# Hybrid mixer trunk on one core: c spread in halves, four spare buffers in the early load ring, 8-step row blocks in the last output groups

## The chip, the cores and the metric

One core of a Trainium2 chip runs the whole program. The metric is device time in microseconds (us), median of several runs. Engines are named as the profile names them: PE (TensorE matmul), PEld (its weight loads), DVE (VectorE), ACT (ScalarE), POOL (GpSimd), SP (SyncE, which here issues the DMAs).

## What is computed

```python
c_act = silu(c)                                   # c: 1 x 2048
for l in range(2):
    mod = c_act @ w_ada[l] + b_ada[l]             # 2048 x 6144: shift, scale, gate
    h = rmsnorm(x, norm_g[l]) * (1 + scale) + shift          # x: 256 x 2048
    z = h @ w_in[l]                               # 2048 x 6656: thirteen pieces of 512
    o_fft = fourier_mix(f_x, w_fft[l]) * silu(f_g)
    o_na = neighbourhood_attention(...) * silu(na_g)
    o_ret = retention(...) * silu(r_g)            # both directions
    o_cv = conformer_conv(...) * silu(cv_g)
    y = concat(o_fft, o_na, o_ret, o_cv) @ w_out[l]          # 2048 x 2048
    x = x + gate * y
return rmsnorm(x, final_g)
```

Inputs and output are float32, and 256 MB of weights are read once.

## The kernel before

**Weights.** The program is a list of steps. A step loads one tile of 128x1024 floats (512 KB, `raw`) by SP. A *weight step* carries two blocks of 128 rows of `w_in` or `w_out`: ACT copies the tile to a rounded half `whi` (L321), DVE forms the remainder `wlo` (L322), and PE multiplies `hh*whi`, `hl*whi` and `hh*wlo`, where `hh` and `hl` are the two halves of the activations. In feature-major groups these are L338, L340, L341 (128x256 out), in row-major groups L367, L368, L369 (128x512 out, once for each half m of the 256 rows). An *ada step* multiplies a tile of `w_ada` (one output block of 128, one half of the 2048 inputs) by `cbc`, the spread silu(c), on DVE and sums it (L468).

**Rings.** `raw` has RAW = 8 buffers and `whi`/`wlo` WB = 4 pairs. Step n's turn issues the load of step n + 8, whose buffer is free when DVE has read it; weights are split up to four weight steps ahead. Each engine then works through its own list in order; a small number of instructions is put ahead by priority (AHEAD = 100), and `prep_x`, `prep_h`, `prep_rows` stand where steps call them.

**Start.** `warm` (L149) keeps PE busy with five matmuls of two passes each; four `cb` matmuls (L153), four tanh on ACT (L155) and four products on DVE (L156) make `cbc`; eight squares on ACT (L200) give the row sums, DVE and POOL make `rstd` (L205 to L207).

**Layer 0 in chunks.** The 16 blocks of 128 features of x are taken as chunks of 2, 3, 5 and 6 blocks (CH0), since a block of h needs its sums of `w_ada` first. While PE multiplies the weights of one chunk, DVE sums the ada tiles of the next. When the last of these is done, `mod_cols` (L1042 to L1044) makes the columns `mcol`, and `prep_h` makes `hh` (ACT, L271), a 32-bit `h` (ACT, L276) and `hl` (DVE, L284) out of the transposed rows `xt` (L231). Weights and ada steps are merged by a fixed rule, and the last few weight steps of a chunk (KEEP) come after all of them.

**Turnover.** `out_steps` makes four groups of 512 output columns. The last four weight steps of the last group form a unit *by rows* (`in_rows`): PE runs all of it for rows m = 0, then for m = 1, with weights kept in buffers of their own (ROW_TAGS). After m = 0, `half(0)` forms `yt` (L441), `xs` (L442) and its square, and then `turn_over(0)` runs: `rms`, and `prep_rows` for layer 1 (xn L243, transposes L245, `hh` L248, h L250 and L252, `hl` L254), while PE multiplies m = 1. The first four weight steps of layer 1 are a unit by rows as well. SPAN says between which weight steps of a stage the ada steps of a later one are placed: for the last out groups of layer 0 from step 1 to 7 before the end.

```python
while n_load < min(len(loads), n_run + RAW):
    loads[n_load].load()
if self is self.unit[-1]:
    g.half(0)
    for w in self.unit:
        w.rows(1)
```

Of the kernel before, what the change touches and what calls it, by code (L numbers as in the profile page):

```python
# [17 lines left out]
P = 128  # L18
# [73 lines left out]
def trunk(ctx, tc, x, c, cols, w_ada, w_in, w_fft, na_bias, consts, conv_w_pw, w_out, final_g, out):  # L92
# [42 lines left out]
    crow = sb.tile([P, DM], F32, tag="gate_bc", name="crow")  # L135
# [3 lines left out]
    nc.sync.dma_start(crow[0:1, :], c)  # L139
# [10 lines left out]
    for j in range(4):  # L150
        sl = slice(j * DG, (j + 1) * DG)
        b = bank("mx", "cb")
        T.matmul(b, one_row[0:1, :], crow[0:1, sl], start=True, stop=True)  # L153
        th = tb("cth")
        A.activation(th, b, AF.Tanh, scale=0.5)  # L155
        V.scalar_tensor_tensor(cbc[:, sl], th, 1.0, b, op0=ALU.add, op1=ALU.mult)  # L156
# [105 lines left out]
    def prep_h_(l, k0, n):  # L262
        for j0 in range(k0, k0 + n, 2):
# [9 lines left out]
            for k in range(w):  # L273
                kt = j0 + k
                if l == 0 or k < H32A:
# [15 lines left out]
    class Step:  # L291
        raw = None
# [3 lines left out]
        def load(self):  # L296
            self.raw = sb.tile([P, 2, DG], F32, tag="raw", name="raw", bufs=RAW)
            stream[0] = nc.sync.dma_start(self.src_view(), self.src)
# [4 lines left out]
    class Weights(Step):  # L303
# [10 lines left out]
        def split(self):  # L314
# [3 lines left out]
            else:  # L318
                self.hi = sb.tile([P, 2, DG], F32R, tag="whi", name="whi", bufs=WB)
                self.lo = sb.tile([P, 2, DG], F32R, tag="wlo", name="wlo", bufs=WB)  # L320
            A.activation(self.hi[:, :n], self.raw[:, :n], AF.Copy)  # L321
# [49 lines left out]
    def in_rows(steps, tags):  # L371

        for s, t in zip(steps, tags):
            s.unit, s.tags = steps, t

    class Group:
# [23 lines left out]
        def half(self, m):  # L400
            pass
# [26 lines left out]
    class OutGroup:  # L428
# [8 lines left out]
        def half(self, m):  # L437
            sl = slice(self.j * DG, (self.j + 1) * DG)
            with tc.high_priority(offset=AHEAD) if self.then else nullcontext():
                t = tb("yt")  # L440
                V.tensor_tensor(t, self.banks[m], GATE[self.l][:, sl], op=ALU.mult)  # L441
# [5 lines left out]
                if self.then:  # L447
                    self.then(m)

# [35 lines left out]
    def spread_gate(l, h):  # L485
# [6 lines left out]
        if h == 0:  # L492
            GATE[l] = sb.tile([P, DM], F32, tag="gate_bc", name="gate_bc")
        nc.gpsimd.dma_start(GATE[l][:, h * KH:(h + 1) * KH],
# [501 lines left out]
    def out_steps(l):  # L996
# [7 lines left out]
        in_rows(ws[-4:], ROW_TAGS[0])  # L1004
# [42 lines left out]
    def mod_chunk(l, k0, n):  # L1047
# [4 lines left out]
        both = mods(l, (0, 1), range(k0, k0 + n), done)  # L1052
# [21 lines left out]
    def turn_over(m):  # L1074
        rms(m)
        prep_rows(1, m, 0, 8)
# [34 lines left out]

    for m in range(2):
        for j in range(4):
            square_piece(m, j)
    rms(0, 1)

    loads = [s for s in steps if isinstance(s, Step)]
    weights = [s for s in steps if isinstance(s, Weights)]
    n_load = n_split = n_run = n_w = 0
    pos = {id(s): i for i, s in enumerate(loads)}  # L1120
    for s in steps:
        if isinstance(s, Step):
            while n_load < min(len(loads), n_run + RAW):
# [113 lines left out]
```

## Time and profile before

| | us |
|---|---|
| median of 3 runs | 974.92 (973.08 to 975.43) |
| the profiled execution | 971.75 |
| its span | 970.0 |
| PE busy | 908.0 |
| DVE busy | 781.3 |
| ACT busy | 591.9 |
| DMA read | 256.61 MB |

The span is what the profile's rows cover; the profiled execution's own time lies 1.75 us above it and 3.17 us under the median of the runs. PE is busy for 94% of the span, so what it loses is spread thin: the table of stretches shows, for each stage, how much of its length PE was not busy. A row of the timeline gives start, duration, engine, line and operation, and in brackets how long the engine had been idle before and what released it. A run of equal matmuls carries one row with its count.

### The profile page before, as it was taken

The page shows a single profiled execution, that of the slowest core. Times are in us where ns is not written, and L with a number is a line of the kernel's source. Part 1 is how long each engine was busy: PE and PEld are TensorE (multiplying, and loading weights), DVE is VectorE, ACT ScalarE, POOL GpSimd, SP SyncE. Part 2 cuts the span into 40 slices and gives each one's busy share as a digit, 9 for nine tenths or more (in the row PEclk, how much of TensorE's full clock was granted, in tenths as well). Part 3 has the DMA queues.
Part 4 walks back from the last instruction along what each step waited for, and adds up shares of the span by engine and source line. Part 5 has one row for each costly group of instructions (what it writes and reads, how often), then busy time and mean ns, then how long its engine had stood idle before and what let it go on. Part 6 is the DMA issues. An engine that isn't in the chain of part 4 may idle for free.

```text
span 970.0 us, 14749 instructions
## 1 busy us (share of the span) xinstructions
PE 908.0 (94%) x5298; PEld 771.2 (80%) x5298; DVE 781.3 (81%) x1269; ACT 591.9 (61%) x1027; POOL 19.6 (2%) x27
## 2 busy tenths in 40 slices
PE   4779799999998998999998999999999999999996
PEld 1668588889996777778886899999977889788784
DVE  5877698878999898987887689557987977578873
ACT  3477574579977766454463545668899844643451
POOL 1000000000000000010000000000000000010000
PEclk7889999999999999999999999999999999999998
DMA  9979899979788578888994799877665576379942
GB/s 348 349 267 335 296 333 354 345 270 347 235 305 292 179 245 291 258 295 314 335 334 146 250 357 396 278 243 233 219 214 178 156 245 229 110 233 320 327 161 87
DMA packets 109067, 259.69 MB, mean 268 GB/s; under 512 B 8385, under 2 KB 10561, under 8 KB 108737
## 3 DMA queue, kind: packets, MB, share of 16 engines
q1 hardware_dynamic: 108290, 256.64, 77.3%
q0 software_dynamic: 704, 2.11, 0.6%
q8 instruction: 41, 0.67, 0.3%
q14 instruction: 32, 0.26, 0.1%
HBM read 256.61 MB, written 2.11 MB: 267 GB/s over the span
## 4 chain that ended last, share of the span: by engine, by line
PE 65%; DVE 16%; DMA 9%; ACT 5%; issue 5%; POOL 1%; DVEq 0%; POOLq 0%; ACTq 0%
PE acc L368 11%; PE acc L367 10%; PE acc L369 10%; PE acc L341 9%; PE acc L338 8%; PE acc L340 8%; DVE wlo L322 6%; DMA raw<-in_w_ada_dram 5%; DVE raw L468 4%; DMA raw<-in_w_in_dram 3%; PE pwb L714 2%; ACT whi L321 1%; DVE cy L642 1%; DVE cy L626 1%; PE ff L810 1%
## 5 line engine op out<-in xcount | busy, mean ns | idle before, releaser
L321 ACT ACTIVATE whi<-raw 128x1024 fp32r<-128x1024 f32 (+1 forms) x272 | 277.1, 1028 | 174.2 <-PE acc L369 88.6
L322 DVE TENSOR_TENSOR wlo<-raw,whi 128x1024 fp32r<-128x1024 f32 (+1 forms) x272 | 319.4, 1181 | 62.1 <-ACT whi L321 60.3
L468 DVE CUSTOM_DVE_ANT_0 raw<-raw,cbc 128x1024 f32<-128x1024 f32 x192 | 232.5, 1219 | 45.5 <-DMA raw<-in_w_ada_dram 45.3
L338 PE MATMUL acc<-hh,whi 128*128 128x256 f32 x896 | 256.1, 287 | 13.4 <-ACT whi L321 6.4
L341 PE MATMUL acc<-hh,wlo 128*128 128x256 f32 x896 | 252.6, 285 | 4.6 <-DVE wlo L322 4.6
L340 PE MATMUL acc<-hl,whi 128*128 128x256 f32 x896 | 253.8, 284 | 1.4 <-DVE hl L284 1.4
L367 PE MATMUL acc<-whi,hh 128*128 128x512 f32 x600 | 241.7, 407 | 3.9 <-ACT whi L321 3.9
L368 PE MATMUL acc<-wlo,hh 128*128 128x512 f32 x600 | 240.2, 400 | 3.2 <-DVE wlo L322 3.1
L369 PE MATMUL acc<-whi,hl 128*128 128x512 f32 x600 | 238.5, 398 | 0.0
L338 PEld LDWEIGHTS acc<-hh,whi 128*128 128x128 f32 x896 | 171.5, 192 | 19.9 <-ACT whi L321 8.1
L341 PEld LDWEIGHTS acc<-hh,wlo 128*128 128x128 f32 x896 | 170.4, 192 | 6.9 <-DVE wlo L322 6.8
L340 PEld LDWEIGHTS acc<-hl,whi 128*128 128x128 f32 x896 | 171.6, 192 | 2.2 <-DVE hl L284 1.7
L367 PEld LDWEIGHTS acc<-whi,hh 128*128 128x128 f32 x600 | 113.6, 190 | 33.5 <-ACT whi L321 4.8
L368 PEld LDWEIGHTS acc<-wlo,hh 128*128 128x128 f32 x600 | 114.2, 190 | 32.7 <-DVE wlo L322 7.2
L369 PEld LDWEIGHTS acc<-whi,hl 128*128 128x128 f32 x600 | 114.0, 190 | 26.2
L417 ACT ACTIVATE z<-acc 128x512 f32<-128x512 f32 x99 | 57.4, 595 | 58.6 <-PE acc L341 31.8
L638 ACT ACTIVATE cvp<-uT,constants 128x256 f32<-128x256 f32 x160 | 70.4, 500 | 11.8 <-DVE cy L642 11.7
L642 DVE TENSOR_TENSOR cy<-cy,cvp 128x512 f32<-128x512 f32 x80 | 52.5, 684 | 1.6 <-ACT cvp L638 1.5
L200 ACT ACTIVATE junk<-xs 128x512 f32<-128x512 f32 x24 | 14.2, 592 | 40.1 <-DVE xs L442 40.1
L392 ACT ACTIVATE acc<-z 128x512 f32<-128x512 f32 x63 | 36.6, 598 | 0.3
L626 DVE SCALAR_TENSOR_TENSOR cy<-uT,constants,cy 128x256 f32<-128x256 f32 x80 | 34.6, 478 | 0.1
L231 PE MATMUL xt<-ident,xn 128*128 128x128 f32 x48 | 8.8, 315 | 11.7 <-DVE xn L226 11.7
(203 smaller groups left out, 703.5 us busy)
## 6 DMA issues: line engine op xcount, KB each, us to landing
raw<-in_w_in_dram SPq DMA_DIRECT2D x198, 512.0 KB, 5.1
raw<-in_w_ada_dram SPq DMA_DIRECT2D x192, 512.0 KB, 5.5
raw<-in_w_out_dram SPq DMA_DIRECT2D x64, 512.0 KB, 5.9
raw<-in_w_in_dram SPq DMA_DIRECT2D x20, 256.0 KB, 5.1
nab<-in_na_bias_dram SPq DMA_DIRECT2D x16, 192.0 KB, 3.6
xs<-in_x_dram SPq DMA_DIRECT2D x2, 1024.0 KB, 5.8
gate_bc<-gate_row POOLq DMA_DIRECT2D x4, 512.0 KB, 5.2
wsm<-in_w_fft_dram SPq DMA_DIRECT2D x4, 512.0 KB, 5.1
```

Of the source, the lines that this page charges most:

```text
L321: A.activation(self.hi[:, :n], self.raw[:, :n], AF.Copy)
L322: V.tensor_tensor(self.lo[:, :n], self.raw[:, :n], self.hi[:, :n].bitcast(F32), op=ALU.subtract)
L338: T.matmul(o, wh[:, sl], hh[:, k], start=fresh and blk % 2 == 0 and blk // 2 not in g.seeded, stop=False, skip_group_check=True)
L340: T.matmul(o, wh[:, sl], hl[:, k], start=False, stop=False, skip_group_check=True)
L341: T.matmul(o, wl[:, sl], hh[:, k], start=False, stop=en, skip_group_check=True)
L367: T.matmul(o, hh[:, k, sl], wh, start=st, stop=False, skip_group_check=m in g.seeded)
L368: T.matmul(o, hh[:, k, sl], wl, start=False, stop=False, skip_group_check=m in g.seeded)
L369: T.matmul(o, hl[:, k, sl], wh, start=False, stop=en, skip_group_check=m in g.seeded)
L417: A.activation(o, i, AF.Copy, scale=0.125 if last and self.piece == NAQ else 1.0)
L468: V.tensor_tensor_reduce(w, w, cbc[:, self.half * KH:(self.half + 1) * KH], 0.5, 0.0, ALU.mult, ALU.add, to)
L638: A.activation(d[:, i], uT[:, b + i, t:t + S], AF.Copy, scale=w[:, t, b + i:b + i + 1])
L642: V.tensor_tensor(y[:, b:b + 2], y[:, b:b + 2], d, op=ALU.add)
```

## The change

Five things:

1. `c` comes in two halves into two tiles of 128x1024, and is spread in two calls, `spread_c(0)` and `spread_c(1)`. The first chunk's ada steps are ordered by half, so that the first ones need only the first half of `cbc`. The warm matmuls go from 5 to 2; the row squares become four of 1024 elements in place of eight of 512, and `rms` is called among the ada steps.
2. `h` of the first chunk (k0 = 0) is made on DVE in place of ACT.
3. The load ring has four spare buffers (SPARE: two tiles of the gate, `yT`, `rk`, all unused so early) up to eight loads before the first step behind layer 0's third chunk (`n_early`). The tile `gate_bc` is split into two halves for it.
4. The last out group's eight weight steps are one unit by rows in place of the last four. The first four of them use the `whi`/`wlo` ring, so `held` puts off a split that would need a buffer of the unit before m = 1 has read it. The transposes for row half 0 of layer 1 are no longer called by `turn_over(0)` but by `between`, after four of the eight steps of m = 1.
5. SPAN of the last out groups goes from (1, 7) to (1, 9).

```diff
-    nc.sync.dma_start(crow[0:1, :], c)
+    for h in range(2):
+        nc.sync.dma_start(crow[h][0:1, :], c[:, h * KH:(h + 1) * KH])
...
+    spread_c(0)
...
-                if l == 0 or k < H32A:
+                if (l == 0 or k < H32A) and (l or k0):
...
+            if self.spare:
+                self.raw = sb.tile([P, 2, DG], F32, tag=self.spare, name="raw")
...
-                    for w in self.unit:
+                    for i, w in enumerate(self.unit):
+                        if i == 4:
+                            g.between()
                         w.rows(1)
+                    self.unit.clear()
...
+    def held(w):
+
+        return w.tags is None and len(ring) >= WB and any(ring[-WB] in u for u in holds)
...
+        def between(self):
+            if self.l < DEPTH - 1:
+                with tc.high_priority(offset=AHEAD):
+                    prep_rows(self.l + 1, 0, 0, 8)
...
-        in_rows(ws[-4:], ROW_TAGS[0])
+        in_rows(ws[-8:], (None,) * 4 + ROW_TAGS[0])
...
+        if k0 == 0:
+            both = [Ada(l, which, k, h) for h in range(2) for k in range(n) for which in range(2)]
+            both[-1].then = done
+            both.insert(2, Call(lambda: spread_c(1)))
+            both.insert(4, Call(lambda: rms(0, 1)))
...
         rms(m)
-        prep_rows(1, m, 0, 8)
+        if m:
+            prep_rows(1, m, 0, 8)
...
+    n_early = pos[id(tail[0])] - RAW
+    for i in range(n_early):
+        r = i % (RAW + len(SPARE))
+        if r >= RAW:
+            loads[i].spare = SPARE[r - RAW]
...
-            while n_load < min(len(loads), n_run + RAW):
+            while n_load < len(loads) and n_load < n_run + RAW + (len(SPARE) if n_load < n_early else 0):
...
-            while n_split < min(len(weights), n_w + WB) and pos[id(weights[n_split])] < n_load:
+            while (n_split < min(len(weights), n_w + WB) and pos[id(weights[n_split])] < n_load
+                   and not held(weights[n_split])):
...
+SPARE = ("gate0", "gate1", "yT", "rk")
...
-SPAN = ((2, 0), (1, 7), (8, 5), (3, 4), (1, 12))
+SPAN = ((2, 0), (1, 9), (8, 5), (3, 4), (1, 12))
-WARM = 5
+WARM = 2
```

How this moves instructions is read at three places. First, DVE at the start of the program, from `cbc` on. `ISA raw,msum<-raw,cbc` is an ada step, `ms` the row sum of `rms`, `xn` the normalized rows of the first chunk. Before:

```order
L156 SCALAR_TENSOR_TENSOR cbc<-cth,cb 128x512 x4
L468 ISA raw,msum<-raw,cbc 128x1024
L468 ISA msum 128x1
L205 TENSOR_REDUCE ms<-ssq 128x1
L206 TENSOR_SCALAR ms<-ms 128x1
L226 TENSOR_SCALAR xn<-xs,rstd 128x256
L468 ISA raw,msum<-raw,cbc 128x1024
```

And now:

```order
L159 SCALAR_TENSOR_TENSOR cbc<-cth,cb 128x512 x4
L210 TENSOR_REDUCE ms<-ssq 128x1
L211 TENSOR_SCALAR ms<-ms 128x1
L231 TENSOR_SCALAR xn<-xs,rstd 128x256
L496 ISA raw,msum<-raw,cbc 128x1024
L496 ISA msum 128x1
L210 TENSOR_REDUCE ms<-ssq 128x1
L211 TENSOR_SCALAR ms<-ms 128x1
L231 TENSOR_SCALAR xn<-xs,rstd 128x256
L496 ISA raw,msum<-raw,cbc 128x1024
```

The row sum and `xn` of the first row half have moved ahead of the first ada step, which still stands behind all four parts of `cbc`.

Second, ACT from the second weight step to the end of chunk 0's weights and on to chunk 1 (`z` and `uT` are evacuations of PE's sums). Before:

```order
L321 ACTIVATE whi<-raw 128x1024
L417 ACTIVATE z<-acc 128x512 x3
L321 ACTIVATE whi<-raw 128x1024
L417 ACTIVATE z<-acc 128x512
...
L417 ACTIVATE z<-acc 128x512 x3
L271 ACTIVATE hh<-xt,mcol 128x256 x2
L276 ACTIVATE h_469<-xt,mcol 128x256 x2
L271 ACTIVATE hh<-xt,mcol 128x256
L276 ACTIVATE h_475<-xt,mcol 128x256
L321 ACTIVATE whi<-raw 128x1024 x4
```

And now:

```order
L330 ACTIVATE whi<-raw 128x1024
L440 ACTIVATE z<-acc 128x512 x3
L330 ACTIVATE whi<-raw 128x1024
L440 ACTIVATE z<-acc 128x512
...
L440 ACTIVATE z<-acc 128x512 x3
L330 ACTIVATE whi<-raw 128x1024
L276 ACTIVATE hh<-xt,mcol 128x256 x2
L281 ACTIVATE h_466<-xt,mcol 128x256 x2
L276 ACTIVATE hh<-xt,mcol 128x256
L281 ACTIVATE h_472<-xt,mcol 128x256
L330 ACTIVATE whi<-raw 128x1024 x3
```

The copies to `whi` stand behind the same evacuations as before, except that the first one of chunk 1 has moved ahead of that chunk's `hh`.

Third, DVE at the turnover, from the split of layer 1's second weight step (`wyT`) to the first `xn` of layer 1. Before:

```order
L322 TENSOR_TENSOR wyT<-raw,wfx 128x1024
L322 TENSOR_TENSOR wlo<-raw,whi 128x1024 x3
L468 ISA raw,msum<-raw,cbc 128x1024
L468 ISA msum 128x1
L322 TENSOR_TENSOR wlo<-raw,whi 128x1024
L468 ISA raw,msum<-raw,cbc 128x1024
L468 ISA msum 128x1
L468 ISA raw,msum<-raw,cbc 128x1024
L468 ISA msum 128x1
L441 TENSOR_TENSOR yt<-acc,gate_bc 128x512
L442 TENSOR_TENSOR xs<-xs,yt 128x512
L468 ISA raw,msum<-raw,cbc 128x1024
```

And now:

```order
L331 TENSOR_TENSOR wyT<-raw,wfx 128x1024
L496 ISA raw,msum<-raw,cbc 128x1024
L496 ISA msum 128x1
L464 TENSOR_TENSOR yt<-acc,gate_bc 128x512
L465 TENSOR_TENSOR xs<-xs,yt 128x512
L331 TENSOR_TENSOR wlo<-raw,whi 128x1024
L210 TENSOR_REDUCE ms<-ssq 128x1
L211 TENSOR_SCALAR ms<-ms 128x1
L248 TENSOR_SCALAR xn<-xs,rstd 128x512
```

Of the three ada steps around `yt` of row half 0 one is left, ahead of it; one `wlo` now stands between `xs` and the row sum.

## Rows read from the trace of the kernel before

**Rows 1.** The page's first part: busy time of each engine, its share of the span, and its instructions.

```profile
PE 908.0 (94%) x5298; PEld 771.2 (80%) x5298; DVE 781.3 (81%) x1269; ACT 591.9 (61%) x1027; POOL 19.6 (2%) x27
```

**Rows 2.** The table of stretches, cut at the stages: chunk 0 (from 26.4), chunk 1, and the tail of layer 0 (262 to 420). Columns: stretch, its length, busy us and instructions of each engine, granted clock of PE as a share of full speed, DMA share, GB/s.

```profile
26.40:58.50 32.10, 22.86 (x144) 20.17 (x144) 24.14 (x45) 16.75 (x28) 0.00 (x0) 0.87 0.94 327
58.50:120.50 62.00, 54.43 (x313) 46.28 (x311) 46.30 (x72) 41.98 (x70) 0.00 (x0) 0.94 0.87 302
262.00:420.00 158.00, 150.41 (x872) 121.39 (x872) 144.95 (x273) 107.33 (x220) 4.08 (x6) 0.98 0.79 267
```

**Rows 3.** The same view for two stretches of 10 us in the early stages.

```profile
50.00:60.00 10.00, 5.85 (x23) 4.17 (x23) 7.57 (x16) 7.17 (x13) 0.00 (x0) 0.81 0.70 239
140.00:150.00 10.00, 10.00 (x86) 9.98 (x85) 8.52 (x14) 4.59 (x7) 0.00 (x0) 1.00 1.04 397
```

**Rows 4.** The view of waits: engine, line, what it waited for, us in total, times, longest. ACT, then PE, from 26.4 to 130; ACT from 130 to 199.1; SP's own queue from 0 to 260.

```profile
ACT z L417 <- PE acc L369: 15.5, 9, 5.1
ACT z L417 <- PE acc L341: 15.0, 9, 3.8
...
PE xt L231 <- DVE xn L226: 4.3, 2, 3.5
PE acc L338 <- ACT whi L321: 4.0, 3, 2.2
...
ACT whi L321 <- DMA raw<-in_w_in_dram: 7.3, 7, 1.9
...
SPq L298 <- DVE wlo L322: 109.6, 70, 5.6
```

**Rows 5.** The timeline at one weight step of chunk 0: start, us, engine, line, operation, and in brackets the idle time before it and its releaser.

```profile
35.98 0.60 ACT L417 ACTIVATE z<-acc 128x512 f32<-128x512 f32 x1 [2.22 <-PE acc L341]
...
36.48 1.05 ACT L321 ACTIVATE whi<-raw 128x1024 fp32r<-128x1024 f32 x1
...
37.58 0.39 PE L338 MATMUL acc<-hh,whi 128*128 128x256 f32 x1 [0.92 <-ACT whi L321]
```

**Rows 6.** The chain of waits, one piece in each line (start, us, what): the first piece after 26 us that is the transfer of a load.

```profile
281.73 5.71 DMA raw<-in_w_in_dram
```

**Rows 7.** The timeline of the start: the warm matmuls, those that spread c, the first ada step, the columns, and chunk 0's first matmuls.

```profile
1.61 6.26 PE L149 MATMUL warm<-warm 128*128 128x512 f32 x10 [1.61 <-DVE warm L146]
...
7.79 3.70 PE L153 MATMUL cb<-crow,one_row 1*128 1x512 f32 x8
...
12.76 1.22 DVE L468 CUSTOM_DVE_ANT_0 raw<-raw,cbc 128x1024 f32<-128x1024 f32 x1
...
25.09 0.16 DVE L1042 TENSOR_TENSOR mcol<-msum 128x4 f32<-128x4 f32 x1
...
26.36 0.80 PE L338 MATMUL acc<-hh,whi 128*128 128x256 f32 x2 [6.07 <-ACT hh L271]
...
28.59 0.58 PE L340 MATMUL acc<-hl,whi 128*128 128x256 f32 x1 [1.44 <-DVE hl L284]
```

**Rows 8.** The timeline at the start of chunk 1.

```profile
54.48 1.02 ACT L271 ACTIVATE hh<-xt,mcol 128x256 fp32r<-128x256 f32 x2
...
57.18 3.92 ACT L321 ACTIVATE whi<-raw 128x1024 fp32r<-128x1024 f32 x4
57.45 1.38 PE L231 MATMUL xt<-ident,xn 128*128 128x128 f32 x5 [3.50 <-DVE xn L226]
...
58.49 1.20 PE L367 MATMUL acc<-whi,hh 128*128 128x512 f32 x2
```

**Rows 9.** The timeline of the turnover: the split `wyT` and SP's two ada loads behind it; the first matmuls of m = 1; DVE's ada steps, `yt`, and `xn`; the transposes, and the matmul that waits for layer 1's first `hl`; the first feature-major matmul of layer 1.

```profile
499.23 1.22 DVE L322 TENSOR_TENSOR wyT<-raw,wfx 128x1024 fp32r<-128x1024 f32 x1
...
500.48 1.47 SPq L298 DMA_DIRECT2D raw<-in_w_ada_dram  x2
...
505.56 1.23 DVE L468 CUSTOM_DVE_ANT_0 raw<-raw,cbc 128x1024 f32<-128x1024 f32 x1 [1.66 <-DMA raw<-in_w_ada_dram]
...
509.68 0.39 PE L367 MATMUL acc<-wnav,hh 128*128 128x512 f32 x1
509.91 0.40 PE L368 MATMUL acc<-wona,hh 128*128 128x512 f32 x1
...
510.46 1.23 DVE L468 CUSTOM_DVE_ANT_0 raw<-raw,cbc 128x1024 f32<-128x1024 f32 x1 [1.39 <-DMA raw<-in_w_ada_dram]
...
511.61 0.69 DVE L441 TENSOR_TENSOR yt<-acc,gate_bc 128x512 f32<-128x512 f32 x1
...
515.78 0.88 DVE L243 TENSOR_SCALAR xn<-xs,rstd 128x512 f32<-128x512 f32 x2 [0.72 <-POOL rstd L207]
516.41 0.63 PE L245 MATMUL xt<-ident,xn 128*128 128x128 f32 x4 [1.96 <-DVE xn L243]
...
517.15 0.63 PE L367 MATMUL acc<-wcvA,hh 128*128 128x512 f32 x1
517.58 0.63 PE L368 MATMUL acc<-wcvU,hh 128*128 128x512 f32 x1
...
522.29 0.50 PE L369 MATMUL acc<-wnaq,hl 128*128 128x512 f32 x1 [1.95 <-DVE hl L254]
...
530.70 0.28 PE L338 MATMUL acc<-hh,whi 128*128 128x256 f32 x1
```

**Rows 10.** The timeline at the end: the last matmul.

```profile
960.22 0.39 PE L369 MATMUL acc<-wcvA,hl 128*128 128x512 f32 x1
```

More of the change, by code (lines that the diff above doesn't have):

```diff
@@ L134, in trunk @@
     xs = sb.tile([P, 2, DM], F32, name="xs")
-    crow = sb.tile([P, DM], F32, tag="gate_bc", name="crow")
+    crow = [wide(t, "crow") for t in ("gate0", "gate1")]
     cbc = sb.tile([P, DM], F32, name="cbc")
@@ L149, in trunk, with spread_c @@
         T.matmul(wb, warm[:, :P], warm, start=True, stop=True)
[L150 to L156, printed above, removed]
+    def spread_c(h):
+        for j in range(2):
+            sl = slice(h * KH + j * DG, h * KH + (j + 1) * DG)
+            b = bank("mx", "cb")
+            T.matmul(b, one_row[0:1, :], crow[h][0:1, j * DG:(j + 1) * DG], start=True, stop=True)
+            th = tb("cth")
+            A.activation(th, b, AF.Tanh, scale=0.5)
+            V.scalar_tensor_tensor(cbc[:, sl], th, 1.0, b, op0=ALU.add, op1=ALU.mult)
+    spread_c(0)
     mbias = pcol[:, 32:96].rearrange("p (l w k) -> p l w k", l=DEPTH, w=2)
@@ L291, in trunk @@
     class Step:
-        raw = None
+        raw = spare = None
         split = None
@@ L296, in load @@
         def load(self):
-            self.raw = sb.tile([P, 2, DG], F32, tag="raw", name="raw", bufs=RAW)
+            if self.spare:
+                self.raw = sb.tile([P, 2, DG], F32, tag=self.spare, name="raw")
+            else:
+                self.raw = sb.tile([P, 2, DG], F32, tag="raw", name="raw", bufs=RAW)
             stream[0] = nc.sync.dma_start(self.src_view(), self.src)
@@ L320, in split @@
                 self.lo = sb.tile([P, 2, DG], F32R, tag="wlo", name="wlo", bufs=WB)
+                ring.append(self)
             A.activation(self.hi[:, :n], self.raw[:, :n], AF.Copy)
@@ L374, in in_rows @@
             s.unit, s.tags = steps, t
+        holds.append(steps)
+    holds = []
+    ring = []
+    def held(w):
+        return w.tags is None and len(ring) >= WB and any(ring[-WB] in u for u in holds)
     class Group:
@@ L400, in half @@
         def half(self, m):
+            pass
+        def between(self):
             pass
@@ L440, in half @@
                 t = tb("yt")
-                V.tensor_tensor(t, self.banks[m], GATE[self.l][:, sl], op=ALU.mult)
+                V.tensor_tensor(t, self.banks[m], GATE[self.l, self.j // 2][:, (self.j % 2) * DG:(self.j % 2 + 1) * DG], op=ALU.mult)
                 V.tensor_tensor(xs[:, m, sl], xs[:, m, sl], t, op=ALU.add)
@@ L448, in half, with between @@
                     self.then(m)
+        def between(self):
+            if self.l < DEPTH - 1:
+                with tc.high_priority(offset=AHEAD):
+                    prep_rows(self.l + 1, 0, 0, 8)
         def done(self):
@@ L491, in spread_gate @@
         nc.gpsimd.dma_start(row, gcol[:, l, 8 * h:8 * h + 8])
-        if h == 0:
-            GATE[l] = sb.tile([P, DM], F32, tag="gate_bc", name="gate_bc")
-        nc.gpsimd.dma_start(GATE[l][:, h * KH:(h + 1) * KH],
+        GATE[l, h] = wide(f"gate{h}", "gate_bc")
+        nc.gpsimd.dma_start(GATE[l, h],
                             bass.AP(tensor=row.tensor, offset=row.offset, ap=[[0, P], [1, KH]]))
@@ L1050, in done @@
             prep_h(l, k0, n)
-        both = mods(l, (0, 1), range(k0, k0 + n), done)
+        if k0 == 0:
[3 more added lines that the diff above has]
+            both.insert(4, Call(lambda: rms(0, 1)))
+        else:
+            both = mods(l, (0, 1), range(k0, k0 + n), done)
         half = len(both) // 2
```

9 lines of the change are left out of this document (5 added, 4 removed).

## The prediction

> **What bounds the kernel now.** I read the engine shares first: PE is busy for 94% of the span [rows 1], so only what PE waits for, or runs at its lower clock, can be won. The table of stretches says where: chunk 0 has 9.2 us without PE (32.10 less 22.86), chunk 1 has 7.6 (62.00 less 54.43), the tail of layer 0 another 7.6, with DVE busy for 92% of it [rows 2]. Then the timeline of the turnover: from the first matmul of m = 1 at 509.68 to the first feature-major one at 530.70 pass 21.02 us, in which PE has 56 matmuls of 0.23 us (509.68 to 509.91) and 16 transposes of about 0.11, together 14.8. So 6.2 us are lost there [rows 9].
>
> The early losses decide what the spare buffers are worth, so I asked who comes last. Up to 130 us ACT waits for PE's sums (15.5 and 15.0 us) and never noticeably for a load; PE waits for ACT's `whi` [rows 4]. At one weight step it can be seen whole: ACT idles 2.22 us for a sum, evacuates it (35.98), and only then copies the next weight (36.48), which PE gets at 37.58 after idling 0.92 [rows 5]. The copy stands *behind the evacuation in ACT's list*. The chain of waits agrees: its first long piece after 26 us that is a load starts at 281.73 [rows 6]. Loads appear as ACT's last arriver only from 130 us on, 7.3 us in all [rows 4], where PE has whole stretches without a gap [rows 3].
>
> **The change part by part.** The sum is made against the profiled execution, 971.75 us, and then carried to the median, 3.17 above it.
>
> *Spread of c, squares, ada order.* Ten warm passes take 6.26 us [rows 7], 0.63 each; six fewer let the `cb` matmuls start up to 3.8 us earlier. Their eight passes take 3.70 at the rate of before; if PE then runs at half that rate, the fourth is done 3.7 later and nothing is won. I take 2, between them, since the warm row itself holds both rates. From that goes what the new order puts ahead of the first ada step: two sums, POOL's `rstd`, `xn`. The same sequence made DVE wait 0.72 for POOL at the turnover and its `xn` is 0.44 [rows 9], so with two short sums about 1.4, an estimate. But before, both such sequences stood among the eight ada steps: from 12.76 to 25.09 pass 12.33 us, and eight steps of the row's 1.22 at most need 9.8 [rows 7]. So 2.5 was spent there already, and now the same work is spent, only earlier. I take the columns 1.5 us earlier (bounds 3.8 and 0). What sets chunk 0 is not the first matmul (26.36) but the wait for `hl` at 28.59 [rows 7], and its `h` is now made on DVE, ahead of `hl`: two operations, each no longer than `xn`'s 0.44 for twice the width, 0.8 together. Term: -0.7, bounds -3 and +0.8. If it fails, the cover is ACT: it is idle there, and the copies wait for nothing else.
>
> *Chunk 1's first copy.* Before, PE idles 3.50 us for `xn`, does five transposes and starts at 58.49, one copy after 57.18, since ACT first did `hh` and `h` from 54.48 on [rows 8]. Now the first copy stands ahead of these and five transposes lie in PE's wait. The first matmul can start up to 2.4 us earlier; the other three copies end when they did, because ACT's work is the same, but the first step's 12 matmuls cover them. Eight transposes now lie behind these 12 matmuls, outside a wait: 0.9 at the price of above, up to 1.4 by the row's 1.38 for five [rows 8]. Term: -1.1, bounds -2.4 and +1.
>
> *Ring of 12.* A load issued earlier takes away a wait for a load. On the chain to 130 us there is none, and ACT's list keeps the copies where they were, behind the same evacuations. What SP waits for (109.6 us for DVE's reads [rows 4]) becomes less, and nobody waits for SP. Term: 0; the bound on the gain is the rival below. Bound on the other side: a spare tile must be free when the gate or the tail needs it; the last spare is used eight loads before that stage, so +0.5 at most.
>
> *Turnover.* m = 1 now has 48 matmuls, 11.2 us, in place of 24. The first transposes stand 21 matmuls (4.9 us) behind its start. DVE's chain to them is `yt` 0.69, `xs` about the same, one `wlo` (1.22, as `wyT`), two sums and the wait for POOL, `xn`: 4.1 us, with hand-offs up to 5.5. So of the 1.96 us of waiting about 0.5 stays: -1.5. The first use of layer 1's `hl` comes 29 matmuls and four transposes (some 7.2 us) behind the first transposes; before it came 5.9 behind and waited 1.95 [rows 9]: -1.7. At the lower clock a matmul takes 0.43 (517.15 to 517.58) in place of 0.23; that cost about 1.8 and goes if the waits get short: 0 to -1.8, I take -0.5. Against this, the same chain for row half 1, with three ada steps among it, now has 24 matmuls (5.6 us) before its transposes and needs 5.4 to 6.9: +1.5. Term: -2.2, bounds -4.5 and +1. What is late next is the ada step ahead of `yt`. Its load waits for the buffer that `wyT` frees: before, `wyT` ended at 500.45 and SP issued the two ada loads from 500.48 on, of which DVE had the first at 505.56 [rows 9], 5.1 us later. Now `wyT` should end about 5.5 us into the pass of m = 0 (four operations of `yt` and `xs` for the group before, 2.8, and two splits, 2.4). The load lands at 10.6, the step ends at 11.8, and `yt` can start at 11.6. It just fits.
>
> *Ends and the rest.* The last group of layer 1 ends with the same m = 1 matmul at 960.22 and the same row sums behind it [rows 10]: 0. Two halves of the gate, consts in one block, SPAN's two steps: off PE's chain, 0.
>
> Sum: -0.7 - 1.1 + 0 - 2.2 = **-4.0 us**: 967.75 for an execution like the profiled one, **971.0** as median (974.92 less 4.0, rounded up).
>
> **The rivals.**
>
> *The loads are the bound early, and the ring opens them.* SP waits most of the early time for a free buffer [rows 4], and the transfers move 327 and 302 GB/s in chunks 0 and 1 [rows 2] where 397 are possible, with 239 in one stretch [rows 3]. The 10.5 and 18.7 MB of these two stretches would pass at 397 in 73.6 us in place of 94.1. PE could give back at most what it idles there, 16.8 us. Then the time is 955 to 962. Against it: no last arriver of that chain is a load [rows 4 to 6]. [...]
>
> *The turnover only trades its waits.* The ada load takes 1 to 3 us more, `yt` and so the transposes come that much later, PE waits 2 to 3 us as before and falls to the lower clock: the turnover's term is 0, and -1.8 stays: 973.1. For it: the fit above has no slack, and the loads' medians differ by more than it. 27%.
>
> *The change doesn't do what it says.* `hl` of chunk 0 comes no earlier because `cb` runs at half rate and `h` loads DVE, the eight transposes cost what the moved copy wins, and the turnover trades waits: 974 to 975.5. 7%.
>
> *The pass of m = 0 drains the splits: slower.* By rows, a weight step lasts 6 x 0.233 = 1.40 us instead of 2.8, and DVE must deliver a remainder in each. If none were ready at the start, DVE would have eight of 1.22, `yt` and `xs` twice (2.8) and two splits of layer 1 (2.4) in 11.2 us: 15.0, so PE loses 3.8, the lower clock adds some 1.4, and in layer 1 the same pass loses 1.4. With the turnover's gain gone and the early -1.8 kept: +4.8, 979.7. It decides at about three remainders ready: then DVE's list fits. Against it: splits run four steps ahead, four of the eight have buffers of their own, and now no ada step lies among them. 9%.
>
> **How the numbers follow.** Forecast 50% (about 968 to 972.5), ring 7%, trade 27%, nothing 7%, slower 9%. I can tell the kernel from no change beyond about 0.3%, 2.9 us: under 972.0 is faster, over 977.8 slower. Faster: 0.46 of the forecast's 0.50, the ring's 0.07, 0.03 of the trade: 0.56. Slower: the drained pass's 0.09, and 0.01 of the rest: 0.10. Same: 0.34. The range leaves out the ring and most of the slow case: 966.0 to 976.0; its low end is the forecast with the turnover at -4.5 and the start at its better half, its high end the case of nothing with half a microsecond more.
>
> **What would show it.** Right: the wait for `hl` at chunk 0 under a microsecond earlier, chunk 1's first matmul 1 to 3 us earlier against the columns, ACT still without a noticeable wait for a load up to 130 us, DMA still near 300 GB/s in chunk 1; at the turnover less than a microsecond before the first transposes, and 56 + 24 matmuls' worth of work with some 4 us lost. Wrong: PE's gaps in chunks 0 and 1 shrink by many microseconds while GB/s rises; `yt` standing behind an ada step that waits for a load; PE waiting for `wlo` in the pass of m = 0.

## The result, and the profile after

969.26 us as median of 18 runs (964.74 to 973.68), against 975.37 for the kernel before (971.51 to 979.89, 18 runs): ratio 0.9935, 95% interval 0.9919 to 0.9951, so 6.1 us less by the medians (4.8 to 7.9 by the interval), where 4.0 were forecast. The profiled execution of after took 973.68 us, more than any other run of it, and that of before 971.75, less than all but one. The two traces are therefore compared stage by stage and not by their ends.

The page's first line of after is the same as that of before [rows 1] within 2 us:

```profile
PE 909.5 (94%) x5292; PEld 770.3 (79%) x5292; DVE 782.2 (80%) x1272; ACT 590.3 (61%) x1017; POOL 19.9 (2%) x27
```

The stretches of [rows 2], after:

```profile
26.40:58.50 32.10, 22.81 (x141) 19.78 (x142) 25.25 (x43) 15.34 (x24) 0.00 (x0) 0.99 1.03 395
58.50:120.50 62.00, 54.53 (x321) 46.13 (x320) 48.40 (x79) 44.39 (x75) 0.00 (x0) 0.95 0.88 310
262.00:420.00 158.00, 149.24 (x866) 119.96 (x866) 145.00 (x272) 107.28 (x220) 4.50 (x6) 0.99 0.80 267
```

In the first stretch the loads do run ahead, 395 GB/s in place of 327, and PE is busy for as long as before, 22.81 us and 22.86. Its clock, 0.99 in place of 0.87, is not to be compared; the last section says why.

The view of waits, ACT from 26.4 to 130, answers to [rows 4]: still the sums of PE, and 0.2 us for a load.

```profile
ACT z L440 <- PE acc L350: 16.6, 9, 5.3
ACT z L440 <- PE acc L381: 12.3, 8, 4.8
...
ACT whi L330 <- DMA raw<-in_w_in_dram: 0.2, 1, 0.2
```

The timeline of the start answers to [rows 7]. The eight `cb` passes last 7.19 us in place of 3.70, the first ada step starts 2.74 us later, the columns stand at 26.06, 0.97 later, and the wait for `hl` ends at 30.56, 1.97 later: PE idles 2.44 for it in place of 1.44, since DVE now makes `h` first. At the next weight step 0.55 comes back: five transposes now lie in PE's wait for `whi`, which is 0.37 in place of 0.92 [rows 5].

```profile
1.61 3.78 PE L150 MATMUL warm<-warm 128*128 128x512 f32 x4 [1.61 <-DVE ssq L1147]
5.32 7.19 PE L156 MATMUL cb<-crow,one_row 1*128 1x512 f32 x8
...
15.50 1.22 DVE L496 CUSTOM_DVE_ANT_0 raw<-raw,cbc 128x1024 f32<-128x1024 f32 x1
...
26.06 0.16 DVE L1069 TENSOR_TENSOR mcol<-msum 128x4 f32<-128x4 f32 x1
...
27.33 0.80 PE L347 MATMUL acc<-hh,whi 128*128 128x256 f32 x2 [8.36 <-ACT hh L276]
27.77 0.99 DVE L284 TENSOR_SCALAR h<-xt,mcol 128x256 f32<-128x256 f32 x2
...
30.56 0.58 PE L349 MATMUL acc<-hl,whi 128*128 128x256 f32 x1 [2.44 <-DVE hl L289]
...
37.81 0.71 PE L236 MATMUL xt<-ident,xn 128*128 128x128 f32 x5
38.88 0.39 PE L347 MATMUL acc<-hh,whi 128*128 128x256 f32 x1 [0.37 <-ACT whi L330]
```

Chunk 1 answers to [rows 8]. One copy now stands ahead of `hh`, and PE waits 1.63 for it, in place of 3.50 for `xn`; the eight transposes, five of which stood ahead of the first matmul, now come behind the first step's matmuls, from 62.02 on.

```profile
55.77 1.05 ACT L330 ACTIVATE whi<-raw 128x1024 fp32r<-128x1024 f32 x1
56.72 1.01 ACT L276 ACTIVATE hh<-xt,mcol 128x256 fp32r<-128x256 f32 x2
56.87 0.74 PE L379 MATMUL acc<-whi,hh 128*128 128x512 f32 x2 [1.63 <-ACT whi L330]
```

The turnover answers to [rows 9]. The one ada step ahead of `yt` is there at 504.58, after DVE idled 5.02 us for its load; `yt` follows at 505.73, 0.25 behind the end of PE's pass of m = 0. This is the order that the prediction gave as a sign of being wrong, but it cost PE little. The first transposes wait 0.51 in place of 1.96, and the first use of `hl`, at 518.53, waits no longer, where it waited 1.95. Two waits are new, both for row half 1 behind its transposes: 0.55 for `hh` and 0.20 for `hl`.

```profile
504.58 1.23 DVE L496 CUSTOM_DVE_ANT_0 raw<-raw,cbc 128x1024 f32<-128x1024 f32 x1 [5.02 <-DMA raw<-in_w_ada_dram]
505.73 0.69 DVE L464 TENSOR_TENSOR yt<-acc,gate_bc 128x512 f32<-128x512 f32 x1
...
510.89 0.63 PE L250 MATMUL xt<-ident,xn 128*128 128x128 f32 x4 [0.51 <-DVE xn L248]
...
518.53 0.39 PE L381 MATMUL acc<-wnaq,hl 128*128 128x512 f32 x1
...
524.97 0.50 PE L379 MATMUL acc<-wnaq,hh 128*128 128x512 f32 x1 [0.55 <-ACT hh L253]
...
526.58 0.50 PE L381 MATMUL acc<-wnaq,hl 128*128 128x512 f32 x1 [0.20 <-DVE hl L259]
```

The table of stretches, from the first matmul of m = 1 to the first feature-major one, in before and then in after: the granted clock was 0.92 and is 1.00, and the second stretch holds 18 more 128x512 matmuls.

```profile
509.68:530.70 21.02, 17.10 (x73) 12.75 (x72) 15.58 (x41) 9.14 (x24) 1.10 (x2) 0.92 0.49 160
```

```profile
505.32:525.54 20.22, 19.16 (x87) 14.87 (x86) 17.89 (x38) 10.96 (x22) 1.96 (x2) 1.00 0.66 203
```

### The profile page after: what moved, and what is told of

The parts are those of the page before. It is cut to its first block, busy times and chain, and to the rows that moved or that the text cites. A ratio compares the mean times of both kernels' runs of the same rounds, so it can differ in the third digit from the quotient of the medians.

```text
span 971.9 us, 14703 instructions
## 1 busy us (share of the span) xinstructions
PE 909.5 (94%) x5292; PEld 770.3 (79%) x5292; DVE 782.2 (80%) x1272; ACT 590.3 (61%) x1017; POOL 19.9 (2%) x27
## 4 chain that ended last, share of the span: by engine, by line
PE 63%; DVE 15%; DMA 10%; issue 6%; ACT 5%; POOL 0%; DVEq 0%; POOLq 0%; ACTq 0%
PE acc L380 10%; PE acc L381 10%; PE acc L379 10%; PE acc L350 9%; PE acc L347 9%; PE acc L349 9%; DVE wlo L331 6%; DMA raw<-in_w_in_dram 4%; DMA raw<-in_w_ada_dram 4%; DVE raw L496 3%; ACT whi L330 2%; PE pwb L741 1%; DMA raw<-in_w_out_dram 1%; PE cb L156 1%; PE ro L930 1%
## 5 line engine op out<-in xcount | busy, mean ns | idle before, releaser
L347 PEld LDWEIGHTS acc<-hh,whi 128*128 128x128 f32 x896 | 169.1, 189 | 21.3 <-ACT hh L276 8.8
L205 ACT ACTIVATE junk<-xs 128x512 f32<-128x512 f32 x16 | 9.5, 593 | 29.5 <-DVE xs L465 29.5
L464 DVE TENSOR_TENSOR yt<-acc,gate_bc 128x512 f32<-128x512 f32 x16 | 10.4, 684 | 12.5 <-PE acc L381 12.5
```

What stands on the lines that cost most here:

```text
L347: T.matmul(o, wh[:, sl], hh[:, k], start=fresh and blk % 2 == 0 and blk // 2 not in g.seeded, stop=False, skip_group_check=True)
```

## Experiments

Two marks from the timelines carry the comparison: **A**, the first matmul of layer 0's second feature-major run of 216 matmuls, 256.88 us in before and 255.98 in after; and **T**, the length from the first matmul of the row-major run that ends layer 0 (the out groups are most of it) to layer 1's first feature-major run of 192, 167.58 in before (389.31 to 556.89) and 166.22 in after. Up to A the two profiles of the changed kernel agree within 0.05 us at each stage's start. Behind it they part: the stage from 283 us on takes 65.08 us in one and 61.62 in the other. What lies there needs several profiles. A itself is not that firm between kernels: turn_ring and turn_ring_l0 run the same instructions up to it, and it stands at 255.74 and 258.29. So where it matters the stretch from chunk 0's first matmul to the second feature-major run of 72 is used as well, 57.10 and 56.98 in these two.

| kernel | median us | ratio to before | 95% interval | A | T |
|---|---|---|---|---|---|
| before | 975.37 | | | 256.88 | 167.58 |
| after | 969.26 | 0.9935 | 0.9919 to 0.9951 | 255.98 | 166.22 |
| after_again | 968.97 | 0.9953 | 0.9931 to 0.9976 | 256.00 | 166.93 |
| turn_alone | 970.14 | 0.996 | 0.9936 to 0.9983 | 256.81 | 166.91 |
| ring_alone | 972.5 | 0.9976 | 0.9953 to 0.9998 | 254.37 | 171.07 |
| start_alone | 975.4 | 1.0022 | 0.9997 to 1.0046 | 259.26 | 173.57 |
| turn_ring | 970.1 | 0.9928 | 0.9902 to 0.9954 | 255.74 | 169.02 |
| after_warm5 | 968.19 | 0.9919 | 0.9892 to 0.9946 | 255.71 | 167.18 |
| before_warm2 | 976.01 | 0.9988 | 0.9955 to 1.0022 | 253.94 | 175.03 |
| turn_ring_l0 | 965.25 | 0.989 | 0.9856 to 0.9924 | 258.29 | 164.65 |
| ring_old_order | 974.4 | 0.9976 | 0.9957 to 0.9994 | 258.03 | 173.22 |
| after_ms_first | 966.66 | 0.9898 | 0.9874 to 0.9923 | 254.58 | 165.57 |
| best_new_start | 967.99 | 0.993 | 0.9899 to 0.9961 | 254.66 | 168.63 |
| best_old_start | 966.93 | 0.9924 | 0.9898 to 0.995 | 258.61 | 167.68 |

Each ratio is against runs of the kernel before on the same chip (medians 973.76 to 976.10).

**The three parts alone.** All three are the changed kernel with the other parts put back; c stays in two transfers. Their ratios multiply to 0.9958, 4.1 us less.

turn_alone:

```diff
     spread_c(0)
+    spread_c(1)
...
-                if (l == 0 or k < H32A) and (l or k0):
+                if l == 0 or k < H32A:
...
+        both = mods(l, (0, 1), range(k0, k0 + n), done)
...
+            square_piece(m, j)
+    rms(0, 1)
...
-SPARE = ("gate0", "gate1", "yT", "rk")
+SPARE = ()
...
-WARM = 2
+WARM = 5
```

> The turnover alone: the last output groups in 8-step row blocks, the transposes called between them, and SPAN (1, 9); the ring stays at 8 and the start is as before (c comes in two transfers, both halves spread at once). My theory: 2.2 us faster than the kernel before (bounds 4.5 faster to 1 slower), and between yt of row half 0 and the first feature-major matmul of layer 1 the loss of 6.2 us falls to about 4. The rival in which the whole gain is the turnover: about 6 us faster. The rival in which the turnover only trades its waits: 0.

Measured 3.9 us less (interval 1.7 to 6.2, which holds the theory's 2.2 and the first rival's 6, and not 0), A unchanged, T shorter. With the block of four steps T is 167.58, 171.07, 173.57, 175.03 and 173.22 us, mean 172.1; with eight in layer 0, nine profiles between 164.65 and 169.02, mean 167.0. The profile that the forecast was made from was the shortest of five and lies among the nine. What splits cleanly is the part of T that the turnover holds, from the last out group's first matmul on: 63.81 (before) to 67.78 with four steps, mean 66.47; 60.84 (after) to 63.33 with eight, mean 61.72. The first transposes wait 1.96 (before) to 4.27 us in the five, 0.51 to 0.63 in the nine.

How the wait grows with four steps is visible in the timeline of before_warm2, whose turnover is that of before. Three ada steps stand around `yt`, and they wait for loads whose buffers come free behind `wyT`. That split ended 9.4 us ahead of the end of PE's pass of m = 0 in before and 7.3 ahead here; the ada step ahead of `yt` waits 1.64 for its load where it waited 1.39, `yt` starts 4.27 us behind the pass in place of 1.77, and the transposes wait 4.27, where [rows 9] had 1.96.

```profile
512.54 1.23 DVE L497 CUSTOM_DVE_ANT_0 raw<-raw,cbc 128x1024 f32<-128x1024 f32 x1 [1.64 <-DMA raw<-in_w_ada_dram]
...
513.69 0.69 DVE L465 TENSOR_TENSOR yt<-acc,gate_bc 128x512 f32<-128x512 f32 x1
...
518.31 1.09 PE L251 MATMUL xt<-ident,xn 128*128 128x128 f32 x4 [4.27 <-DVE xn L249]
```

With eight steps one ada step is left there. DVE idles 4.8 to 6.1 us for its load in the nine profiles, and `yt` starts 0.04 to 1.29 us behind the pass; the wait is 0.63 in turn_alone, with the latest `yt`, and 0.56 in after_ms_first. It did not follow the load.

ring_alone has the start as above, SPARE as changed, and the turnover of before:

```diff
-        in_rows(ws[-8:], (None,) * 4 + ROW_TAGS[0])
+        in_rows(ws[-4:], ROW_TAGS[0])
...
-        if m:
-            prep_rows(1, m, 0, 8)
+        prep_rows(1, m, 0, 8)
...
-SPAN = ((2, 0), (1, 9), (8, 5), (3, 4), (1, 12))
+SPAN = ((2, 0), (1, 7), (8, 5), (3, 4), (1, 12))
```

> The four spare buffers alone, with the start and the turnover as before. My theory: 0 (within 1 us), since ACT's copies stand behind the same evacuations and none of them waits for a load up to 130 us. The rival in which loads bound the early stages: 4 us faster or more, with the gaps of PE in chunks 0 and 1 shorter and more GB/s in chunk 1 than 302.

Neither. By the ratio 2.3 us are won (0.2 to 4.6), and A is 2.5 us earlier (254.37), more than the theory and less than the rival had. Nor does the rival's way of winning show: chunk 0's stretch has 388 GB/s and the same three waits of PE for `whi`, 0.92 each, and chunk 1's has 310. What differs is the list: ACT's first copy of chunk 1 is ahead of `hh` here too.

```profile
55.21 1.05 ACT L331 ACTIVATE whi<-raw 128x1024 fp32r<-128x1024 f32 x1
56.16 1.01 ACT L277 ACTIVATE hh<-xt,mcol 128x256 fp32r<-128x256 f32 x2
56.31 0.73 PE L380 MATMUL acc<-whi,hh 128*128 128x512 f32 x2 [1.63 <-ACT whi L331]
```

A split is issued only for a weight whose load has been issued (`pos < n_load`); a longer ring lets it be issued earlier, and so puts it earlier in ACT's list.

start_alone keeps the new start, with that turnover and SPARE empty:

> The start alone: c spread in halves, the order of the first ada steps, two warm matmuls, the squares of 1024 elements, h of chunk 0 on DVE, and the copy ahead of chunk 1's hh if it comes with them; ring of 8, turnover as before. My theory: 1.8 us faster (bounds 4 faster to 1 slower), the columns of chunk 0 1.5 us earlier. The rival in which the start is worth nothing, because PE runs at its lower clock through the spread of c and DVE has h to make: 0, with the columns no earlier than before.

The rival has it: the `cb` passes ran at their low rate (7.19 us), the columns are 0.97 later, and the ratio, 1.0022, doesn't exclude zero. A is 2.4 us *later*: 0.97 at the columns, 1.0 at the first `hl`, less the 0.55 of the next weight step, and 0.8 in four feature-major runs behind 85 us, whose equal matmuls are slower (see Addresses).

after_again (no edit):

> The changed kernel once more, for a second profile, since the first one on record is 4 us above its median. If the theories of the three parts are right and add up, it is as fast as the sum of the three parts alone, about 6 us under the kernel before. A place where the first profile was late and this one is not is chance; a place where both are late is the program.

Its ratio's interval, 2.3 to 6.7 us less, holds both 4.0 and 6.1, and the 4.1 of the three parts. At A the two profiles agree within 0.02 us; the first one's late places, from 283 us on, are chance by the rule of the expectation.

**Loads or list.** ring_old_order has the ring of 12, but splits are issued as with 8:

```diff
-            while (n_split < min(len(weights), n_w + WB) and pos[id(weights[n_split])] < n_load
+            while (n_split < min(len(weights), n_w + WB) and pos[id(weights[n_split])] < min(n_load, n_run + RAW)
```

> The ring of 12 alone as in the run with the ring alone, but a weight may be split only when a ring of 8 would have let it: the loads run ahead with 12 buffers, while ACT's and PE's lists up to 130 us are again those of the kernel before. Theory A (the ring's gain of 2.5 us up to 256 us is the place of chunk 1's first copy in ACT's list, not the loads): PE's first matmul of the second feature-major run of 72 stands at about 85.5, half a microsecond behind the kernel before (85.01) as its start does, and by 256 us nothing is won. Rival B (earlier loads are what helps): 83.5 there and 254.4 at the run of 216, as with the ring alone.

85.55 and 258.03: theory A. The lists of PE and ACT are those of before up to 150 us. From chunk 0's first matmul to that run pass 58.86 us, 58.66 in before and 56.61 in ring_alone; over all profiles 58.1 to 59.3 in the five with the copy behind `hh`, 56.4 to 57.5 in the nine with it ahead. With 385 GB/s in chunk 0, PE waits for `xn` at chunk 1 as in [rows 8], and ACT's copies are again behind `hh`:

```profile
54.94 1.02 ACT L277 ACTIVATE hh<-xt,mcol 128x256 fp32r<-128x256 f32 x2
...
57.63 3.93 ACT L331 ACTIVATE whi<-raw 128x1024 fp32r<-128x1024 f32 x4
57.91 1.38 PE L237 MATMUL xt<-ident,xn 128*128 128x128 f32 x5 [3.50 <-DVE xn L232]
```

Its ratio is nevertheless as low as ring_alone's, 0.9976, with an interval (0.9957 to 0.9994) that leaves out 1. So beyond A something of the longer ring may help (the tail of layer 0 starts with more loads issued); the spread of single profiles there hides it, and it stays open.

**The start.** turn_ring puts the whole start back, as in the first edit above, and keeps ring and turnover:

> The changed kernel with the start put back as it was: c spread at once, five warm matmuls, eight squares, h of chunk 0 on ACT, ada steps in their old order; ring of 12 and turnover as changed. Theory A (the start costs some 2 us, the ring's gain is chunk 1's copy that moves ahead of hh, the turnover gives 2 to 4): faster than the changed kernel by 1 to 3 us, 6 to 9 under the kernel before; the ring's 2.5 us at 256 us into the span stand in the trace in full, not the 0.9 of the changed kernel. Rival B (the start is worth nothing either way, its late columns are made up for by the ring): as fast as the changed kernel, within 1 us.

0.9928: it can't be told from the changed kernel, so theory A's 1 to 3 us are not shown and rival B is not excluded. A is 255.74, not 254.4: here the passes of the five warm matmuls were slow for longer (7.50 us in all) and the columns stood at 26.33, 0.74 later than in ring_alone, which is about half of the difference. after_warm5 and before_warm2 change one number:

```diff
-WARM = 2
+WARM = 5
```

> The changed kernel with five warm matmuls in place of two, nothing else. Theory A (the two warm matmuls end before PE's passes get short, so the eight cb passes take 0.86 us each and push the first ada step behind): the cb passes take 0.43 each again, the columns of chunk 0 come 0.5 to 1.5 us earlier than 26.06. A second point: in the profiles of kernels with the new start, long stretches of equal matmuls later on (614 to 694 us) take 81.45 us in place of 80.54. If that comes from the number of PE's instructions ahead, it goes here; if it comes from another part of the start, it stays at 81.45.

The columns come at 25.36, 0.70 earlier, and the `cb` passes take 0.43 each. The stretch of 672 stays at 81.45.

> The kernel before (with c in two transfers) with two warm matmuls in place of five. Theory A: cb passes at 0.86 us each, chunk 0's columns 1 to 2 us later than 25.09, and the time 1 to 2 us longer. Rival B (the warm matmuls can go, the spread of c has slack behind the squares): columns at 25.1, same time. The second point as in the run with five: 81.45 or 80.54 us from the first of the 672 equal matmuls to the next row-major group.

A miss: here two warm matmuls were *better* in the profile, and the time, 0.9988, is the same. The `cb` passes started at 5.32 as in after and took 3.82 us in all, and the columns stood at 24.12. (The edit is one number, but DVE's list moved with it: the row sum and `xn` now stand ahead of the first ada step here too.) So two warm matmuls are a matter of chance. PE's passes begin at 0.85 us and become 0.43 at a moment that differs from profile to profile; where it came before the end of `cb`, it came between 5.0 and 7.6 us, and the two warm matmuls end at 5.3. Of seven profiles with two, `cb` ran at 0.43 in two (before_warm2, after_ms_first) and at 0.85 in five (after twice, start_alone, best_new_start, best_old_start); with five warm matmuls it ran at 0.43 in all seven. In the five slow ones PE was busy from 1.61 to 12.51 us without the change; why is open. The timeline's row of `cb`, in best_new_start and then in after_ms_first:

```profile
5.32 7.19 PE L156 MATMUL cb<-crow,one_row 1*128 1x512 f32 x8
```

```profile
5.32 3.86 PE L156 MATMUL cb<-crow,one_row 1*128 1x512 f32 x8
```

**Addresses.** In the four profiles with the new start as changed (after twice, start_alone, after_warm5), equal matmuls were slower later on: from the first of the 672 to the next row-major group 81.45 us, against 80.54 in the others. after_ms_first moves addresses alone:

```diff
+    small("ms", 1)
     junk = wide("nak", "junk")
```

> The changed kernel with the four small tiles ms given their place in memory ahead of the tile for the squares, as they had before. No instruction changes and none moves; only the addresses of raw, whi and wlo move by 128 bytes, so that they stand to hh and hl as in the kernel before (modulo 4096). Theory A (the 1% by which equal matmuls are slower in the four profiles with the new start comes from the addresses): 80.54 us from the first of the 672 equal matmuls to the next row-major group, 57.31 for the stretch before, and 2 to 3 us less in all. Rival B (it comes from something else in the new start): 81.45 and 57.66 to 57.76, same time as the changed kernel.

80.54 and 57.31, as theory A had it, and 0.9898: no instruction differs. (The time is not the addresses' alone to show: best_new_start below, with the same addresses, is at 0.993.) The timelines of after, then of after_ms_first, at both ends of the stretch:

```profile
612.00 0.28 PE L347 MATMUL acc<-hh,whi 128*128 128x256 f32 x1
...
693.45 0.40 PE L379 MATMUL acc<-whi,hh 128*128 128x512 f32 x1
```

```profile
607.48 0.28 PE L347 MATMUL acc<-hh,whi 128*128 128x256 f32 x1
...
688.02 0.39 PE L379 MATMUL acc<-whi,hh 128*128 128x512 f32 x1
```

**Versions.** turn_ring_l0 keeps the block of eight in layer 0 only:

```diff
-        in_rows(ws[-8:], (None,) * 4 + ROW_TAGS[0])
+        n = 4 if l else 8
+        in_rows(ws[-n:], (None,) * (n - 4) + ROW_TAGS[0])
```

> As the run with ring and turnover alone, but the 8-step row block only in layer 0; layer 1's last group keeps its block of four. Theory A: the last group of layer 1 gains nothing from eight steps and in two profiles PE waited 0.5 us in it for a remainder, so this is 0 to 0.7 us faster than the one with both. Rival B (the earlier end of row half 0 shortens the output's end): 1 us slower or more.

0.989 against 0.9928, intervals that overlap; the output stage is as long as in turn_ring within half a microsecond (121.97 and 122.44 from the last row-major run's start to the last matmul). What the smaller block is worth is not shown. The last pair joins what had seemed to pay.

best_new_start is after_ms_first with the edit above and

```diff
-                if (l == 0 or k < H32A) and (l or k0):
+                if l == 0 or k < H32A:
```

> The kernel with ms placed first, and two parts of the change taken back: h of chunk 0 is made on ACT again, and layer 1's last output group is a block of four steps again. Theory A: PE's wait for the first hl, 2.85 us between the second and third matmul of chunk 0 in four profiles with h on DVE, is 1.85 again; the last group loses nothing; 0.5 to 2 us under the kernel with ms first alone (966.66), 10 to 12 under the kernel before. Rival B (the moved h frees ACT for the copies, and the block of eight in layer 1 is of use): no faster than with ms first alone.

best_old_start is turn_ring_l0 with

```diff
-WARM = 5
+WARM = 2
```

> Ring of 12, the 8-step block in layer 0 alone, the old order of the start, but two warm matmuls. Theory A (the order of the first ada steps is worth nothing, PE's rate through the spread of c is what counts): within 1.5 us of the other kernel of this pair. Rival B (spreading c in halves pays): the other one is more than 1.5 us faster. In both, the cb passes take 0.43 or 0.85 us each as the case may be in the profiled execution, with the columns at 24 or 26.

PE's wait for the first `hl` is 1.44 again in best_new_start (the 1.85 of the expectation, which counts from the matmul before), but the median is no lower than with ms first alone: that part of theory A is not borne out. In both profiles the `cb` passes took 0.85 us, and chunk 0's first matmul stood at 27.33 and 28.76, the columns at 26.06 and 27.49:

```profile
26.06 0.17 DVE L1070 TENSOR_TENSOR mcol<-msum 128x4 f32<-128x4 f32 x1
```

```profile
27.49 0.16 DVE L1071 TENSOR_TENSOR mcol<-msum 128x4 f32<-128x4 f32 x1
```

So at an equal rate of `cb`, and with two warm matmuls in both, the new start is 1.43 us earlier; at the other rate, after_ms_first (23.40) is 0.72 ahead of before_warm2 (24.12). The medians are within 1.1 us, and a gain of that size can't be told in them. Of all versions after_ms_first, 0.9898 with its upper end at 0.9923, and turn_ring_l0, 0.989 and 0.9924, gain most and can't be told apart; the first is one line away from the change.

## Why the prediction was right, and where it was not

The direction and the range held, and the forecast's 4.0 is less than the first comparison's interval (4.8 to 7.9) and inside the second's (2.3 to 6.7). Of the four terms the start's had the wrong sign, and the copy's and the turnover's were too small.

*Start, -0.7: wrong in sign.* The step that failed is the 2 us taken between full and half rate of `cb`. In this execution all eight passes ran at half rate, the lower bound, and ended 1.02 later than before (12.51, 11.49). The sequence for `xn` was only moved, as forecast: from there to the first ada step 1.72 more, from that step to the columns 1.77 less (10.56, 12.33). So the columns are 0.97 later. What cost was the rate: at an equal rate and with as many warm matmuls the new start was 1.43 and 0.72 us ahead (above). The second half, `h` on DVE, was taken as 0.8 and measured 1.0 (2.44 less 1.44), of which 0.55 comes back one weight step on; that return was not in the sum. Alone, the start costs 2.4 us at A. What I had not seen: since `rms` is first called among the steps, the four `ms` tiles get their place behind the load buffers, and raw, whi and wlo lie 128 bytes off. That is 0.8 of the 2.4, and some 3 us more behind T (81.45 less 80.54 in one stretch, 0.45 in the stretch before, 0.5 in the one behind 749 us, about 1.2 in the last).

*Chunk 1's first copy, -1.1: right in mechanism, undersized, and put to no edit.* From chunk 0's first matmul to the run of 72 at 85 us pass 56.61 us in ring_alone and 58.66 in before, 2.05 less; in ring_old_order 58.86. The copy moves because the ring is longer, which the sum, with the ring at 0, did not have.

*Ring, 0: right about the early loads, wrong about lists.* The rows named ACT's list and not the loads, and the run with the loads ahead but the list of before gains nothing at A. The 2.3 us that this run gains in time are not explained. The rival "the loads are the bound" (16.8 us) did not happen: no gap of PE in chunk 0 shrank in ring_alone. The sentence "ACT's list keeps the copies where they were" held for chunk 0 and failed at chunk 1, against the term before it. Nor did four more buffers with the list of before shorten the gap of [rows 5]: in ring_old_order, at 385 GB/s in chunk 0, PE idles 0.92 us for ACT's copy at 38.06 as it did at 37.58.

*Turnover, -2.2: right in mechanism, a term mis-sized.* Each wait came out close: 0.51 where 0.5 was left, nothing where some 0.25 was, the new ones 0.55 and 0.20 where 1.5 was taken. The granted clock of the stretch is 1.00, where before had 0.92, so the 1.8 put to the lower clock went whole, where 0.5 was taken. In the two profiles themselves the part from the last out group on is 2.97 shorter (63.81, 60.84), near the term. But the loss before was taken from one profiled execution, 6.2 us, where four other profiles of the same turnover were 2.2 to 4.0 us longer in this part and 3.5 to 7.5 in T. By the means the gain is 4.75 in this part (66.47 less 61.72) and 5.1 in T (172.1 less 167.0). These are single profiles of different kernels, so chance and kernel are not told apart. Some of it was visible ahead, in the 1.39 and 0.54 that DVE waited for ada loads around `yt`, the first in [rows 9] and the second here:

```profile
513.56 1.23 DVE L468 CUSTOM_DVE_ANT_0 raw<-raw,cbc 128x1024 f32<-128x1024 f32 x1 [0.54 <-DMA raw<-in_w_ada_dram]
```

*Sum.* -0.9 at A, about -5.1 in T, and some 3 back by the addresses behind it: about -3. By the medians the two comparisons of the changed kernel give 6.1 us less (interval 4.8 to 7.9) and 4.8 (2.3 to 6.7), so two to three microseconds are not placed; they may lie in the stages behind 283 us, where profiles of one kernel differ by as much. That the forecast's 4.0 came near is in part luck: two errors of opposite sign, the start's and the turnover's.

The rival of a drained pass happened in part. In the pass of m = 0 PE waited for remainders for 0.5 us in after and up to 3.0 among the nine profiles with eight steps (turn_ring, in the two waits below), where the rival had 3.8; it never ate up the turnover's gain:

```profile
495.90 0.50 PE L381 MATMUL acc<-wlo,hh 128*128 128x512 f32 x1 [1.12 <-DVE wlo L332]
...
499.43 0.50 PE L381 MATMUL acc<-wlo,hh 128*128 128x512 f32 x1 [1.87 <-DVE wlo L332]
```

## What to carry to other kernels

Before a wait is priced from one profiled execution, ask what it hangs on. A wait at the end of a chain of loads and splits can be a spread (1.96 to 4.27 us in five profiles here), and removing it is worth its mean. When the issue of work is tied to the number of buffers, more buffers can change the order of instructions as well as the traffic: here the stretch from chunk 0's first matmul to the run of 72 took 58.66 us before, 56.61 with both (ring_alone), and 58.86 with the traffic alone (ring_old_order). Compare the lists, and test each alone. A tile that is asked for at another place, however small, can shift all the others; here a stretch of equal matmuls in both profiles shows it (81.45 against 80.54 us).

## What the runs showed of the hardware

Equal 128x256 matmuls took 1.1% longer (81.45 us in after against 80.54 in after_ms_first for the stretch of 672) when raw, whi and wlo lay 128 bytes off their former place relative to hh and hl, with the same instructions; why was not tested. PE's first passes of 512 columns start 0.85 us apart (2.62, 3.48 and 4.33 in after) and later ones 0.43 (5.56, 5.99 and 6.42 in before). In nine profiles the rise came 5.0 to 7.6 us after the start, in the warm passes (ten took 6.23 us in all in turn_alone, 7.50 in turn_ring) or the first `cb` pass (eight took 3.82 in before_warm2, 3.86 in after_ms_first). In the other five all eight `cb` passes took 0.85. In after, one of these, chunk 0's matmuls start 0.21 us apart up to 33.93 and 0.12 apart from 34.11 on.

The clock column does not show this early low rate. In after the trace's first record of the clock begins at 34.06 us, in before at 5.06, both where PE's rate rises; ahead of it the column reads 1.00, so in the stretch of after from 4.30 to 8.00, which holds five passes where that of before holds nine. For chunk 0's first matmuls, which start 0.21 us apart in both kernels, it reads 1.00 in after and 0.50 in before, where a record of 0.5 runs from 11.89 to 32.37. The rows are after, after, and before:

```profile
4.30:8.00 3.70, 3.70 (x5) 1.16 (x4) 0.00 (x0) 0.57 (x1) 0.00 (x0) 1.00 0.99 415
26.00:32.00 6.00, 2.23 (x8) 1.94 (x9) 5.89 (x14) 2.08 (x3) 0.00 (x0) 1.00 1.04 409
```

```profile
26.00:32.00 6.00, 4.21 (x18) 3.92 (x19) 6.00 (x13) 2.61 (x5) 0.00 (x0) 0.50 1.02 383
```
